# Separate in and out buffers on GpSimd's queue, state copies on VectorE, other PSUM banks for transposes, and a new order of scaling, tables and weights in a hybrid diffusion block

## The chip, the cores and the metric

The kernel runs on one core of a Trainium2 chip. The metric is device microseconds for one execution of the whole program; three runs of the kernel before took 2377.81 to 2379.08 us, with a median of 2378.53. Engines in the profile: PE is TensorE's matmul and PEld its weight load, DVE is VectorE, ACT is ScalarE, POOL is GpSimd, SP is SyncE, which issues nearly all DMAs here.

## The reference

One layer over 2048 latent tokens of 1024 channels and 256 context tokens, all float32. A token mixer comes first, then a channel mixer:

```python
sh1, sc1, g1, sh2, sc2, g2 = modulation(c, w_mod, b_mod)           # silu(c) @ w_mod + b_mod
zc = modulate(rmsnorm(hc, norm1_g), csh1, csc1) @ w_in             # context
zx = modulate(rmsnorm(h, norm1_g), sh1, sc1) @ w_in                # latent: S5 part, conv part
stx_f = s5_scan(ux, disc_f, h0_f, False)                           # 32 groups of 16, 64 complex states
stx_b = s5_scan(ux, disc_b, h0_b, True)                            # starts from the context's state
mix = concatenate([s5_mixer(ux, stx_f, stx_b, ...),                # C h + D u, GELU, GLU
                   conformer_conv(zx[..., 512:], ...)])            # GLU, depthwise conv 31, LayerNorm, swish
h = h + g1 * (mix @ w_out)
h = h + g2 * conv_ffn(h, ...)   # up to 2 x 2816, depthwise conv 3 and SiLU on the gate, product, down
return rmsnorm(h, final_g)
```

## The kernel before

Activations lie with channels on the partitions, in four tiles q = 0 to 3 of 512 tokens. Each float32 matmul is made of three float32r matmuls (`mm3`): weight and input are split into a high part, cast by ScalarE (`wH`, `x0H`, `x1H`), and a low part, the difference, by VectorE (`wL`, `x0L`, `x1L`). One output tile of 128x512 with an inner size of 512 is twelve matmuls.

The work is in stages.

Stage 1, to about 310 us. `xload` and `xstat` (together `stat(q)`) load a tile and find its reciprocal root mean square; `xapply` (`app(q)`, lines 235 to 247) scales it on VectorE and splits it. `s5_pass` and `conf_block` multiply by `w_in`. Meanwhile VectorE builds the S5 tables: 16 calls of `win_tab` (products at line 427, transposed by PE into the cv banks, written to `WI_d`) and 8 of `wall_tab` (line 452, to `WA_d` and `KC_d`). `win_tabs(n)` makes the next n of the 16. The order of these calls is at lines 686 to 703.

Stage 2, to about 470 us. The S5 input matmuls (line 755), VectorE's scan over blocks of 16 steps (lines 788 to 791), the rest of the modulation (`mod_block`, streamed `w_mod`) and of `conf_block`.

Stage 3, to about 670 us. 16 rounds, one for each pair of groups: eight copies of states from `S` into `h0` and `h1` (lines 838 and 842; buffers named hr, two of each), eight matmuls into an ax bank (lines 847 to 850), a copy of the bank into `yt` (line 855); after each fourth round PE transposes `yt` and ScalarE applies GELU (lines 861 to 863). Three steps of the convolution `conv_all` are taken after each round: `conv_in` transposes the gated input (line 561), `conv_mm` multiplies by banded Toeplitz tiles (line 575), `conv_out` transposes back (line 589). S5 and the convolution's transposes take turns in the same two ax banks.

Stage 4, to about 735 us. `mix_glu` for four tiles, and `layer_norm` over the convolution's output.

Stage 5, to about 990 us. `out_half(n, qs, ts_)` multiplies the mix by one half of `w_out`, over eight output blocks m and two tiles q: 64 tiles in all. For each, `xb` (three buffers) takes the residual (for n = 0 from the input, for n = 1 the partial sum `P_d`), VectorE adds the gated product in place, and GpSimd's queue stores it to `P_d` or `H_d`. `t_prep` (pass 0) runs beside the third `out_half`: from `H_d` it makes the seven operands T of a Strassen-like product and writes them to `T_d`; `t_load` reads and splits them.

Stage 6, from about 990 to 1866 us. Two passes p of 22 `unit`s. A unit loads and combines its weights (`left`: two loads into `wr`, which has four buffers, four splits, four sums), then makes seven products (`prod`) of twelve matmuls in the order B11, T2, B21, T1, T3, B22, T4. In the last unit of pass 0 each product is followed by `t_load` of the same operand for pass 1.

Stage 7, to the end. The down projection (`down`, line 1129), which adds into the held tiles, and the final norm.

The context is made with `schedule_with_timeline_sim=True`: a planner in the compiler orders the instructions on each engine and the DMAs on each queue by an estimate of when each is ready, with the order of the program as priority. So neighbours in the program need not be neighbours in the trace; but once laid out, each engine and each queue runs its list in order, and an instruction that waits holds up all behind it.

Of the kernel before, what the change touches and what calls it, by code (L numbers as in the profile page):

```python
# [9 lines left out]
FT = mybir.dt.float32  # L10
# [34 lines left out]
def tile_block(ctx, tc, xl, cxl, wmod, cols, s5p, dcol, eye, win, wglu, wout, wup, wdn, toep, out):  # L45
# [22 lines left out]

    def ps_ax():
        return pp_["ax"].tile([128, 512], FT, name="ax")  # L70

    def ps_fl():
        return pp_["fl"].tile([128, 512], FT, name="fl")
# [341 lines left out]
    def win_tab(d, gb):  # L415
        g0 = d * 32 + gb * GB
        wt = tbu.tile([128, 1024], FT, name="wt", bufs=1)
        for i, g2 in enumerate((g0, g0 + 2)):
            ta = tbu.tile([128, 2, 256], FT, name="wa", bufs=2)
            tc_ = tbu.tile([128, 2, 256], FT, name="wb", bufs=1)  # L420
            x = []
            for tl, lam, bb in ((ta, LR, BA), (tc_, LI, BB)):
                e = lam[:, 0:16, g2:g2 + 2].rearrange("p e g -> p g e")
                if d == 1:
                    e = e[:, :, ::-1]
                o = tl[:, :, :256]
                V.tensor_tensor(o.rearrange("p g (c e) -> p g e c", e=16),
                                e.unsqueeze(3).to_broadcast([128, 2, 16, 16]),
                                bb[:, g2:g2 + 2, :].unsqueeze(2).to_broadcast([128, 2, 16, 16]), op=OP.mult)
                x.append(o)  # L430
            V.tensor_tensor(x[0], x[0], x[1], op=OP.add)
            ps = pp_["cv"].tile([128, 512], FT, name="cv")
            for g in range(2):
                for k in range(2):
                    TE.transpose(ps[:, (g * 2 + k) * 128:(g * 2 + k + 1) * 128],  # L435
                                 ta[:, g, k * 128:(k + 1) * 128], ident)
            A.copy(wt[:, i * 512:(i + 1) * 512], ps)
        SY.dma_start(WI_d[d, gb], wt)
# [113 lines left out]
    def conv_in(n, q, gt):  # L552


        g2 = wp.tile([128, 1024], FT, name="wr", bufs=4)
        SY.dma_start(g2, G_d[q, n])
        for h in range(2):
            pt = ps_ax()
            for r in range(4):
                o = (4 * h + r) * 128  # L560
                TE.transpose(pt[:, r * 128:r * 128 + 128], g2[:, o:o + 128], ident)
            A.copy(gt[:, 8 * q + 4 * h:8 * q + 4 * h + 4, :], pt.rearrange("p (r i) -> p r i", r=4))
            yield
# [19 lines left out]
    def conv_out(n, co, las):  # L583

        for q in range(NQ):
            for h in range(2):
                pt = ps_ax()
                for r in range(4):
                    TE.transpose(pt[:, r * 128:r * 128 + 128], co[:, :, 8 * q + 4 * h + r], ident)
                for s in range(2):  # L590
                    A.activation(las[q][:, 2 * n + s, 256 * h:256 * h + 256].rearrange("p (r w) -> p r w", w=W),
                                 pt.rearrange("p (r s w) -> p s r w", r=4, s=2)[:, s], AF.Identity,
                                 bias=col("cb", 2 * n + s))
                yield
# [16 lines left out]
    def layer_norm(q, hs):  # L611
# [1 line left out]
        a = las[q]  # L613

        def col_mean(f):
            w = cf.tile([128, 2, TQ], FT, name="pt", bufs=2)
            V.tensor_tensor(w, f(0), f(1), op=OP.add)
            ts_ = cf.tile([128, TQ], FT, name="lsum", bufs=1)
            V.tensor_tensor(ts_, w[:, 0], w[:, 1], op=OP.add)
# [63 lines left out]
    def app(q, x, rb):  # L683
        X[q] = xapply(q, *x, rb)
# [1 line left out]
    cr = ctx_mm(ctx_scale(*xc, rbc, 0))  # L686
    app(2, x2, rb2)
    s3 = stat(3)
    win_tabs(2)
    ctx_out(cr)  # L690
    app(3, *s3)
    s0 = stat(0)
    win_tabs(4)
    s5_pass((2, 3))
    s1 = stat(1)
    win_tabs(4)
    for j in range(4):
        conf_block(j, (2, 3))
    app(0, *s0)
    app(1, *s1)  # L700
# [39 lines left out]
    for gb in range(NB):  # L740
# [7 lines left out]
        for i in range(2):  # L748
            a = gb * 2 + i
            for d in range(2):  # L750
                ps = ps_ax() if d == 0 else pp_["cv"].tile([128, 512], FT, name="cv")
                for ri in range(2):
                    for k in range(2):
                        for b in range(2):
# [62 lines left out]
    for a in range(16):  # L817
# [17 lines left out]
        h0 = so.tile([128, 2, NL], FT, name="hr0", bufs=2)  # L835
        for ri in range(2):
            for b in range(2):
                A.copy(h0[ri * 64:ri * 64 + 64, b, :], S[b * 64:b * 64 + 64, 0, a, ri, NC_ - 1:NC_ - 1 + NL])
        h1 = so.tile([128, 2, NL], FT, name="hr1", bufs=2)
        for ri in range(2):  # L840
            for b in range(2):
                A.copy(h1[ri * 64:ri * 64 + 64, b, :], S[b * 64:b * 64 + 64, 1, a, ri, 1:1 + NL])  # L842
        ps = ps_ax()
        for g in range(2):
            o = ps[:, g * 256:(g + 1) * 256]
# [77 lines left out]
    def out_half(n, qs, ts_):  # L923
# [3 lines left out]
        for m in range(KT):  # L927
# [4 lines left out]
                wh, wl = split_w(wr)  # L932
            o = 512 * (m % 2)
            for q, t in zip(qs, ts_):
                xb = lp.tile([128, TQ], FT, name="xb", bufs=3)
                SY.dma_start(xb, (P_d if n else xl)[q, :, m, :])
                ps = ps_mm()
                for k in range(4):
                    c = slice(o + 128 * k, o + 128 * k + 128)
                    mm3(ps, wh[:, c], wl[:, c], t[:, 0, k], t[:, 1, k], k == 0, k == 3)  # L940
                V.scalar_tensor_tensor(xb, ps, mod[:, 16 + m, 0:1], xb, op0=OP.mult, op1=OP.add)  # L941
                P.dma_start((H_d if n else P_d)[q, :, m, :], xb)  # L942
                if n == 0:
                    continue
# [90 lines left out]
    def left(i):  # L1035
# [16 lines left out]
        vs = split(v[:, 512:])  # L1052
        return gs_, s12s, s34s, vs

    def unit(i, p, nxt=None):
        gw, s12, s34, vw = left(i)

        def prod(ps, w, o, b, first=True, last=True):
            wh, wl = w
# [6 lines left out]
                TE.matmul(ps, lhsT=wl[:, c], rhs=t[:, 0, k], start=False, stop=e, skip_group_check=True)  # L1066
            if nxt is not None:
                t_load(nxt, b)

        def new(name, bufs):  # L1070
            return po.tile([128, TQ], FT, name=name, bufs=bufs)
# [258 lines left out]
```

## Time and profile before

| | before |
|---|---|
| median of three runs | 2378.53 us |
| the profiled execution, its own time | 2375.49 us |
| its span, first to last instruction | 2373.7 us |
| PE busy | 2198.7 us (93%) |
| PEld busy | 1758.8 us (74%) |
| VectorE busy | 1638.5 us (69%) |
| ScalarE busy | 830.9 us (35%) |
| GpSimd busy | 49.9 us (2%) |
| mean granted TensorE clock | 0.957 |
| DMA traffic | 349.7 MB, 147 GB/s in the mean |

The profile is that of one execution, whose time of its own is 3.0 us under the median; outside the span lie 1.8 us. Busy PE says that a matmul was in flight, not that it ran at its peak: the clock says at which of its two levels it ran. Times in the rows are microseconds from the start of the span, unless ns is said.

### The profile page before, as it was taken

The numbers are of one execution on the slowest core, as the hardware profiler recorded it, in microseconds if no ns is written. First come the engines' busy times: TensorE is split into PE (matmuls) and PEld (weight loads), VectorE is DVE, ScalarE is ACT, GpSimd is POOL, SyncE is SP. The second block draws the span as 40 slices with busy tenths as digits, with TensorE's granted clock in tenths as the row PEclk, the third lists the DMA queues.
The fourth block names the chain that finished last, engine by engine and source line by source line (L and its number), as shares of the span: only waits on it lengthen the run. The fifth ranks groups of instructions, "written<-read, shape, count | busy, mean of one in ns | idle before, by whom it ended". The sixth has DMA issues, their size and how long they took to land.

```text
span 2373.7 us, 28855 instructions
## 1 busy us (share of the span) xinstructions
PE 2198.7 (93%) x10958; PEld 1758.8 (74%) x10958; DVE 1638.5 (69%) x2506; ACT 830.9 (35%) x1221; POOL 49.9 (2%) x83
## 2 busy tenths in 40 slices
PE   6899999887887967899999997999999999999996
PEld 3678777576765845688778886888888888888885
DVE  9893578830256566677697768777777787788775
ACT  3452311145364433343343344333333311132113
POOL 0000000000000101100000000000000000000002
PEclk9999999979798978899999998999999999999998
DMA  8552586676424679522363234222222732334311
GB/s 321 177 153 89 143 276 228 228 223 185 129 90 172 204 261 318 197 80 89 116 213 97 80 110 148 89 85 83 91 80 80 265 126 80 106 107 144 105 54 71
DMA packets 178683, 349.70 MB, mean 147 GB/s; under 512 B 54512, under 2 KB 82544, under 8 KB 178032
## 3 DMA queue, kind: packets, MB, share of 16 engines
q1 hardware_dynamic: 173424, 331.07, 43.0%
q0 software_dynamic: 5120, 16.78, 1.8%
q8 instruction: 86, 1.41, 0.2%
q14 instruction: 53, 0.43, 0.1%
HBM read 252.45 MB, written 95.35 MB: 147 GB/s over the span
## 4 chain that ended last, share of the span: by engine, by line
issue 65%; PE 23%; DMA 5%; ACT 3%; DVE 2%; POOL 1%; SPq 0%; POOLq 0%; ACTq 0%; DVEq 0%
PE mm L182 5%; PE mm L183 4%; PE mm L184 4%; PE mm L575 2%; PE ax L847 1%; PE cv L755 1%; DMA xb<-P_d 1%; PE ax L755 1%; DMA xr<-in_xl 1%; PE ax L154 1%; PE fl L468 1%; ACT hr L842 1%; POOL P_d L942 1%; PE ax L849 1%; PE cv L435 1%
## 5 line engine op out<-in xcount | busy, mean ns | idle before, releaser
L183 PE MATMUL mm<-bh,bd 128*128 128x512 f32 (+1 forms) x720 | 277.4, 385 | 0.0
L184 PE MATMUL mm<-bh,bd 128*128 128x512 f32 (+1 forms) x720 | 277.1, 385 | 0.0
L182 PE MATMUL mm<-bh,bd 128*128 128x512 f32 (+1 forms) x720 | 274.4, 386 | 0.0
L1064 PE MATMUL mm<-t,wH 128*128 128x512 f32 x528 | 207.9, 394 | 18.0 <-ACT wH L1031 17.4
L1066 PE MATMUL mm<-t,wL 128*128 128x512 f32 x528 | 207.4, 393 | 0.5 <-DVE wL L1032 0.5
L1065 PE MATMUL mm<-t,wH 128*128 128x512 f32 x528 | 207.0, 392 | 0.0
L183 PEld LDWEIGHTS mm<-bh,bd 128*128 128x128 f32 x720 | 135.3, 188 | 27.4 <-issue 0.7
L182 PEld LDWEIGHTS mm<-bh,bd 128*128 128x128 f32 x720 | 135.3, 188 | 27.3 <-DVE x1H L1129 0.2
L184 PEld LDWEIGHTS mm<-bh,bd 128*128 128x128 f32 x720 | 135.3, 188 | 27.0 <-issue 0.2
L1116 ACT CAST bd<-wr 128x1024 fp32r<-128x1024 f32 x44 | 46.2, 1050 | 306.2 <-PE mm L184 296.1
L1031 ACT CAST wH<-sr 128x1024 fp32r<-128x1024 f32 x88 | 92.6, 1054 | 164.0 <-PE mm L1065 143.8
L1032 DVE TENSOR_TENSOR wL<-sr,wH 128x1024 fp32r<-128x1024 f32 x88 | 107.4, 1221 | 55.7 <-ACT wH L1031 55.7
L183 PE MATMUL mm<-x0L,wH 128*128 128x512 f32 (+1 forms) x352 | 139.6, 397 | 0.2 <-DVE x0L L494 0.2
L182 PE MATMUL mm<-x1H,wH 128*128 128x512 f32 x320 | 130.7, 408 | 8.3 <-DVE xb L941 8.3
L1064 PEld LDWEIGHTS mm<-t,wH 128*128 128x128 f32 x528 | 100.4, 190 | 39.8 <-ACT wH L1031 18.2
L184 PE MATMUL mm<-x1H,wL 128*128 128x512 f32 x320 | 128.2, 401 | 0.0
L1031 ACT CAST wH<-wr 128x1024 fp32r<-128x1024 f32 (+1 forms) x88 | 73.6, 837 | 154.4 <-PE mm L1065 143.3
L1066 PEld LDWEIGHTS mm<-t,wL 128*128 128x128 f32 x528 | 100.1, 190 | 22.8 <-DVE wL L1032 1.9
L1065 PEld LDWEIGHTS mm<-t,wH 128*128 128x128 f32 x528 | 100.3, 190 | 20.8
L1100 DVE TENSOR_TENSOR c<-mm,u 128x512 f32<-128x512 f32 x44 | 30.4, 691 | 120.8 <-PE mm L1066 120.7
L1129 DVE SCALAR_TENSOR_TENSOR x1L<-mm,mod,x1L 128x512 f32<-128x512 f32 (+1 forms) x96 | 66.9, 705 | 42.5 <-PE mm L184 42.5
L1129 DVE SCALAR_TENSOR_TENSOR x0L<-mm,mod,x0L 128x512 f32<-128x512 f32 x88 | 65.5, 750 | 41.3 <-PE mm L184 41.2
(349 smaller groups left out, 4980.1 us busy)
## 6 DMA issues: line engine op xcount, KB each, us to landing
wr<-in_wup SPq DMA_DIRECT2D x88, 512.0 KB
Y_d<-ft SPq DMA_DIRECT2D x88, 256.0 KB
wr<-in_wdn SPq DMA_DIRECT2D x44, 512.0 KB
wr<-Y_d SPq DMA_DIRECT2D x44, 512.0 KB
mw<-in_wmod SPq DMA_DIRECT2D x32, 512.0 KB
wr<-T_d SPq DMA_DIRECT2D x28, 512.0 KB
wr<-in_win SPq DMA_DIRECT2D x26, 512.0 KB
u<-U_d SPq DMA_DIRECT2D x32, 288.0 KB
```

Of the source, the lines that this page charges most:

```text
L182: TE.matmul(ps, lhsT=wh, rhs=xh, start=first, stop=False)
L183: TE.matmul(ps, lhsT=wh, rhs=xlo, start=False, stop=False)
L184: TE.matmul(ps, lhsT=wl, rhs=xh, start=False, stop=last)
L575: TE.matmul(pp[s][r, 32 * i:32 * i + 32], lhsT=tv[r, i, :], rhs=gt[r, :, 16 * c + i], start=True, stop=True, tile_position=(64 * s, 64 * s ...
L755: sil = TE.matmul(ps[64 * b:64 * b + 64, ri * NK:(ri + 1) * NK], lhsT=wi[d][:, 2 * i + b, k, ri * 64:(ri + 1) * 64], rhs=u[:, k, 2 * i + b ...
L1031: A.copy(h[:, :n], raw)
L1032: V.tensor_tensor(l[:, :n], raw, h[:, :n].bitcast(FT), op=OP.subtract)
L1064: TE.matmul(ps, lhsT=wh[:, c], rhs=t[:, 0, k], start=f, stop=False, skip_group_check=True)
L1065: TE.matmul(ps, lhsT=wh[:, c], rhs=t[:, 1, k], start=False, stop=False, skip_group_check=True)
L1066: TE.matmul(ps, lhsT=wl[:, c], rhs=t[:, 0, k], start=False, stop=e, skip_group_check=True)
L1116: A.copy(t[:, 0], wr)
L1129: V.scalar_tensor_tensor(h, ps, mod[:, 40 + m, 0:1], h, op0=OP.mult, op1=OP.add)
```

## The change

It has five parts:

- `out_half` loads the residual into buffers `xi` of their own (three), on GpSimd's queue instead of SP's, and VectorE writes the sum into `xb` (now two buffers), which is stored as before. `pt` of `layer_norm` has one buffer instead of two.
- The copies of states into `h0` and `h1` are VectorE's instead of ScalarE's.
- The transposes of `conv_in` and `conv_out` go to the two cv banks instead of the two ax banks. (`ps_cv` is a name for what was written out.)
- In stage 1, `app(3)` is followed by `s5_pass((2, 3))`, which has no tables ahead of it any more; `stat(0)` comes after that, and `win_tabs` are spread by twos between the calls of `conf_block`. The number of tables is the same.
- In the last unit of pass 0, the weights of unit 0 of pass 1 (`left(0)`) are prepared right after the second product and its `t_load`, and handed over through the list `pre`.

```diff
@@ -68,6 +68,9 @@
 
     def ps_ax():
         return pp_["ax"].tile([128, 512], FT, name="ax")
+
+    def ps_cv():
+        return pp_["cv"].tile([128, 512], FT, name="cv")
 
     def ps_fl():
         return pp_["fl"].tile([128, 512], FT, name="fl")
@@ -429,7 +432,7 @@
                                 bb[:, g2:g2 + 2, :].unsqueeze(2).to_broadcast([128, 2, 16, 16]), op=OP.mult)
                 x.append(o)
             V.tensor_tensor(x[0], x[0], x[1], op=OP.add)
-            ps = pp_["cv"].tile([128, 512], FT, name="cv")
+            ps = ps_cv()
             for g in range(2):
                 for k in range(2):
                     TE.transpose(ps[:, (g * 2 + k) * 128:(g * 2 + k + 1) * 128],
@@ -555,7 +558,7 @@
         g2 = wp.tile([128, 1024], FT, name="wr", bufs=4)
         SY.dma_start(g2, G_d[q, n])
         for h in range(2):
-            pt = ps_ax()
+            pt = ps_cv()
             for r in range(4):
                 o = (4 * h + r) * 128
                 TE.transpose(pt[:, r * 128:r * 128 + 128], g2[:, o:o + 128], ident)
@@ -584,7 +587,7 @@
 
         for q in range(NQ):
             for h in range(2):
-                pt = ps_ax()
+                pt = ps_cv()
                 for r in range(4):
                     TE.transpose(pt[:, r * 128:r * 128 + 128], co[:, :, 8 * q + 4 * h + r], ident)
                 for s in range(2):
@@ -613,7 +616,7 @@
         a = las[q]
 
         def col_mean(f):
-            w = cf.tile([128, 2, TQ], FT, name="pt", bufs=2)
+            w = cf.tile([128, 2, TQ], FT, name="pt", bufs=1)
             V.tensor_tensor(w, f(0), f(1), op=OP.add)
             ts_ = cf.tile([128, TQ], FT, name="lsum", bufs=1)
             V.tensor_tensor(ts_, w[:, 0], w[:, 1], op=OP.add)
@@ -686,15 +689,18 @@
     cr = ctx_mm(ctx_scale(*xc, rbc, 0))
     app(2, x2, rb2)
     s3 = stat(3)
-    win_tabs(2)
     ctx_out(cr)
     app(3, *s3)
+    s5_pass((2, 3))
+    win_tabs(2)
     s0 = stat(0)
-    win_tabs(4)
-    s5_pass((2, 3))
+    conf_block(0, (2, 3))
+    win_tabs(2)
+    conf_block(1, (2, 3))
+    win_tabs(2)
     s1 = stat(1)
-    win_tabs(4)
-    for j in range(4):
+    for j in (2, 3):
+        win_tabs(2)
         conf_block(j, (2, 3))
     app(0, *s0)
     app(1, *s1)
@@ -748,7 +754,7 @@
         for i in range(2):
             a = gb * 2 + i
             for d in range(2):
-                ps = ps_ax() if d == 0 else pp_["cv"].tile([128, 512], FT, name="cv")
+                ps = ps_ax() if d == 0 else ps_cv()
                 for ri in range(2):
                     for k in range(2):
                         for b in range(2):
@@ -835,11 +841,11 @@
         h0 = so.tile([128, 2, NL], FT, name="hr0", bufs=2)
         for ri in range(2):
             for b in range(2):
-                A.copy(h0[ri * 64:ri * 64 + 64, b, :], S[b * 64:b * 64 + 64, 0, a, ri, NC_ - 1:NC_ - 1 + NL])
+                V.tensor_copy(h0[ri * 64:ri * 64 + 64, b, :], S[b * 64:b * 64 + 64, 0, a, ri, NC_ - 1:NC_ - 1 + NL])
         h1 = so.tile([128, 2, NL], FT, name="hr1", bufs=2)
         for ri in range(2):
             for b in range(2):
-                A.copy(h1[ri * 64:ri * 64 + 64, b, :], S[b * 64:b * 64 + 64, 1, a, ri, 1:1 + NL])
+                V.tensor_copy(h1[ri * 64:ri * 64 + 64, b, :], S[b * 64:b * 64 + 64, 1, a, ri, 1:1 + NL])
         ps = ps_ax()
         for g in range(2):
             o = ps[:, g * 256:(g + 1) * 256]
@@ -932,13 +938,14 @@
                 wh, wl = split_w(wr)
             o = 512 * (m % 2)
             for q, t in zip(qs, ts_):
-                xb = lp.tile([128, TQ], FT, name="xb", bufs=3)
-                SY.dma_start(xb, (P_d if n else xl)[q, :, m, :])
+                xi = lp.tile([128, TQ], FT, name="xi", bufs=3)
+                P.dma_start(xi, (P_d if n else xl)[q, :, m, :])
                 ps = ps_mm()
                 for k in range(4):
                     c = slice(o + 128 * k, o + 128 * k + 128)
                     mm3(ps, wh[:, c], wl[:, c], t[:, 0, k], t[:, 1, k], k == 0, k == 3)
-                V.scalar_tensor_tensor(xb, ps, mod[:, 16 + m, 0:1], xb, op0=OP.mult, op1=OP.add)
+                xb = lp.tile([128, TQ], FT, name="xb", bufs=2)
+                V.scalar_tensor_tensor(xb, ps, mod[:, 16 + m, 0:1], xi, op0=OP.mult, op1=OP.add)
                 P.dma_start((H_d if n else P_d)[q, :, m, :], xb)
                 if n == 0:
                     continue
@@ -1052,8 +1059,10 @@
         vs = split(v[:, 512:])
         return gs_, s12s, s34s, vs
 
+    pre = []
+
     def unit(i, p, nxt=None):
-        gw, s12, s34, vw = left(i)
+        gw, s12, s34, vw = pre.pop() if pre else left(i)
 
         def prod(ps, w, o, b, first=True, last=True):
             wh, wl = w
@@ -1066,6 +1075,8 @@
                 TE.matmul(ps, lhsT=wl[:, c], rhs=t[:, 0, k], start=False, stop=e, skip_group_check=True)
             if nxt is not None:
                 t_load(nxt, b)
+                if b == T2:
+                    pre.append(left(0))
 
         def new(name, bufs):
             return po.tile([128, TQ], FT, name=name, bufs=bufs)
```

## Rows read from the trace of the kernel before

**Rows 1.** Page, part 1: busy time, share of the span and instructions by engine.
```profile
PE 2198.7 (93%) x10958; PEld 1758.8 (74%) x10958; DVE 1638.5 (69%) x2506; ACT 830.9 (35%) x1221; POOL 49.9 (2%) x83
```
**Rows 2.** Stretches: length, busy time of each engine, TensorE clock, DMA share, GB/s.
```profile
86.00:108.00 22.00, 14.09 (x55) 9.51 (x56) 20.01 (x32) 10.49 (x19) 0.00 (x0) 0.77 0.69 183
...
471.00:530.00 59.00, 52.69 (x600) 47.59 (x600) 24.92 (x50) 26.00 (x64) 0.00 (x0) 0.71 0.74 229
530.00:669.00 139.00, 112.79 (x882) 94.63 (x883) 22.45 (x27) 67.59 (x184) 0.00 (x0) 0.86 0.47 145
...
757.00:773.00 16.00, 9.10 (x22) 4.84 (x21) 10.33 (x14) 9.19 (x10) 0.54 (x1) 0.68 0.71 240
...
879.00:905.00 26.00, 19.23 (x69) 15.23 (x69) 17.51 (x25) 7.48 (x10) 2.65 (x5) 0.81 1.02 358
905.00:948.00 43.00, 33.27 (x129) 25.43 (x128) 26.21 (x27) 18.82 (x20) 5.17 (x11) 0.92 0.88 301
...
1422.00:1446.00 24.00, 8.54 (x26) 6.12 (x27) 21.60 (x26) 14.18 (x17) 0.00 (x0) 0.72 0.77 246
1446.00:2348.00 902.00, 901.32 (x4027) 746.81 (x4026) 676.82 (x919) 269.47 (x342) 0.20 (x1) 1.00 0.31 102
```
**Rows 3.** PE's waits, whole span: who waited for whom, us, times, longest.
```profile
PE mm L182 <- ACT wH L172: 26.6, 4, 15.0
...
PE mm L182 <- DVE xb L941: 13.9, 8, 3.4
...
PE ax L561 <- ACT x0H L562: 5.3, 3, 2.7
...
PE ax L861 <- ACT yt L855: 4.4, 4, 1.5
...
PE ax L589 <- ACT yt L855: 3.5, 4, 1.1
```
**Rows 4.** Chain of waits that ended last, near 81 us: start, length, what.
```profile
81.29 7.14 DMA xr<-in_xl
```
**Rows 5.** VectorE in order of time, 80 to 97 us: start, length, what.
```profile
81.99 0.17 DVE L118 RECIPROCAL stt<-stt 128x4 f32<-128x4 f32 x1
...
96.69 0.75 DVE L235 SCALAR_TENSOR_TENSOR xr<-xr,gs,ax 128x512 f32<-128x512 f32 x1
```
**Rows 6.** Line 838 alone (842 is alike): ns min/median/max.
```profile
L838 ACT COPY hr<-S x64: 294/297/300, 473.7 to 654.6; 64x128 f32<-64x128 f32 x64
```
**Rows 7.** VectorE's copies of lines 763 and 764: ns min/median/max.
```profile
L763 DVE COPY S<-cv x16: 417/422/426, 316.1 to 374.6; 128x256 f32<-128x256 f32 x16
L764 DVE COPY S<-cv x16: 179/181/184, 316.5 to 375.0; 128x32 f32<-128x32 f32 x16
```
**Rows 8.** SP queue's waits, 735 to 990 us: us, times, longest.
```profile
SPq L936 <- DMA H_d<-xb: 74.2, 29, 6.6
SPq L936 <- DMA P_d<-xb: 64.1, 22, 6.9
```
**Rows 9.** SP queue in order of time, 735 to 775 us, merged.
```profile
735.47 26.84 SPq L936 DMA_DIRECT2D xb<-in_xl  x11
762.41 8.28 SPq L930 DMA_DIRECT2D wr<-in_wout  x6
```
**Rows 10.** Line 942 alone, GpSimd's stores: ns each; landing in us.
```profile
L942 POOL DMA_DIRECT2D P_d<-xb x32: 539/539/710, 739.6 to 937.0; - x32
...
DMA to landing us min/median/max: 2.2/3.6/7.0
```
**Rows 11.** PE in order of time at the pass change; idle before it, releaser.
```profile
1440.45 0.79 PE L1064 MATMUL mm<-t,wH 128*128 128x512 f32 x1 [14.32 <-ACT wH L1031]
```
**Rows 12.** VectorE in order of time at the pass change.
```profile
1439.16 1.23 DVE L1021 TENSOR_TENSOR x1L<-wr,x1L 128x1024 fp32r<-128x1024 f32 x1 [1.78 <-ACT x1L L1020]
```
**Rows 13.** VectorE by line, 1400 to 1462 us: count, busy us, mean ns.
```profile
L1032 DVE TENSOR_TENSOR wL<-sr,wH 128x1024 fp32r<-128x1024 f32 x4 | 4.9, 1224 | 0.6 <-ACT wH L1031 0.6
...
L1045 DVE TENSOR_TENSOR sr<-wr 128x512 f32<-128x512 f32 x3 | 2.1, 687 | 0.0
```

## The prediction, made before the changed kernel ran

> **What bounds the kernel now.** The page's first part comes first: TensorE (PE) is busy for 2198.7 us of a span of 2373.7, VectorE for 69%, ScalarE for 35%, GpSimd for 2% [rows 1]. So PE sets the end, and what can be won is its idle time, 2373.7 - 2198.7 = 175 us, and what it does at the lower clock. The table of stretches says where that lies [rows 2]: from 1446 to 2348 us PE stands still for 0.7 us of 902, so nothing that only lightens another engine there is worth anything. That row also gives the pace, 4027 matmuls in 902 us, 0.224 us each at the full clock, so 2.69 us for a tile of twelve. The holes lie in five places: 86 to 108 us (22.0 - 14.1 = 7.9 us idle), 471 to 530 (6.3), 530 to 669 (26.2), 735 to 998 (the output projection; 6.9 us in the stretch from 757 to 773 and 9.7 in that from 905 to 948 alone), and 1422 to 1446 (15.5). The rest, at the start, the tail and in small pieces between, isn't touched. PE's list of waits names who ended the holes [rows 3], and I take the edits by those names.
>
> **Scaling ahead of tables (86 to 108 us).** Edit: app(3) and the first s5_pass come ahead of the first two win_tabs, and stat(0) behind s5_pass. Nothing is removed; all 16 win_tabs stay to be done somewhere. In the chain of waits a load for stat(0) runs from 81.3 to 88.4 us [rows 4]; ScalarE and VectorE then finish that statistic while PE's next matmuls wait, although they need only tile 3's rsqrt. VectorE began that rsqrt at 81.99 and the scaling by it at 96.69, with tables and stat(0) between [rows 5]. The four small steps and two transposes need some 3 us by themselves, so up to 10 us could come forward. The hole is 7.9 us, and at a mean clock of 0.77 the 14.1 us of work in it lose about 14.1 x 0.23 = 3 more: at most 11. Against it: the order on each engine is a planner's, which fills VectorE with tables whenever it thinks it free, wherever they are written. I take 6, bounds -6 (the same hole again, elsewhere) and 11.
>
> **Copies on VectorE, transposes in other banks (471 to 669 us).** ScalarE loses 128 copies of 0.297 us [rows 6], 38 us of the 93.6 that it is busy in the two stretches [rows 2]. Eight of them, 2.4 us, stand in each of the 16 rounds around the copy of yt out of PSUM, and PE waits for yt and for the convolution's copies by name: 5.3 + 4.4 + 3.5 us in the three largest rows [rows 3]. The 3.5 (a convolution transpose that waits for S5's yt) is purely the shared pair of ax banks, and goes with the new banks. Of the 5.3, ScalarE's copies in the way are most; of the 4.4 (yt itself) two thirds. Then 3.5 + 4 + 3 = 10.5; smaller waits of the same kind and clock regained (0.86 in that stretch) give 2.5. I take 13 of the 32.5 us idle; bounds 5 (the bank wait and little else) and 20. VectorE's price is not in the trace for this shape: between 0.18 us (128x32) and 0.42 us (128x256, out of PSUM) [rows 7]; I take 0.25, nearer the small one, since 128 elements lie nearer to 32. That is 32 us, bounds 23 and 54, beside 47 us of work in 198, so VectorE's idle time hides it. Were that cover gone, the matmuls that read the copies would be late, and then yt.
>
> The Trainium skill has a price for these copies (VectorE: DVE Perf Modes, section The TRN2 errata): 58 cycles and one per element at 0.96 GHz, as an estimate 0.19 us for 128 elements; for ScalarE its 224 and one per element at 1.2 GHz come to 0.293, and the trace shows 0.297. By it VectorE would get 25 us more, not 32, and the sum would be the same.
>
> **Loads on GpSimd's queue, buffers of their own (735 to 998 us).** Before, one of three buffers xb holds a load, the sum and the store, and the load goes out on SP's queue only once an earlier store has landed: SP stands waiting for stores of xb for 74.2 + 64.1 = 138 us [rows 8], and everything behind stands too. From 735.47 on eleven such loads take 26.8 us of the queue, and only then are the next weights of wout asked for, at 762.41 [rows 9]. PE's hole from 757 to 773 ends with those weights. After, the eleven are elsewhere; the weights can be there before PE is. Idle 6.9 us, and 9.1 us of work at a clock of 0.68 loses about 3: I take 8, bounds 3 and 10.
>
> From 905 to 948 PE waits for xb itself (most of the 13.9 us that it waits for it in all [rows 3]). A load there waits for a landing. After, it waits only for the sum that last read its buffer, and the store has two buffers: sum 0.75, issue 0.3, landing 3.6 in the middle and 7.0 at worst [rows 10], halved: 2.3 to 4.0 us a tile, against 2.69 for PE. At about 5.3, between the two, it is 3.2. Ten tiles went by in 43 us, 4.3 each; ten times 1.1 is 11. The DMA share is 0.88 there, so I take 7, bounds 0 and 11. PE's longest wait for wout's weights, 15.0 of 26.6 us [rows 3], lies between these two stretches, from 863 to 878, but there SP's queue is full of t_prep's stores and the DMA share is 1.02 from 879 to 905 [rows 2]; I take 3, bounds 0 and 12. The rest of the stage, 2. Together 20, bounds 3 and 32. GpSimd gets 64 issues of 0.539 us [rows 10], 35 us, hidden by its idleness. That col_mean has one buffer costs nothing: both steps that use it are VectorE's, in order.
>
> **left(0) early (1422 to 1446 us).** PE starts pass 1 at 1440.45 after 14.3 us of waiting for wH [rows 11], so pass 0 ended at 1426.1. The weights' load stands behind the reloads of all seven T tiles in the same four buffers. After, it is asked for after the second. Then what is late next is the last T tile: its split ended at 1440.39 [rows 12], and before it now stand four splits, one of half width, and four sums of left(0), about 3 x 1.22 + 0.7 + 4 x 0.69 = 7.1 us [rows 13], so 1447.5. PE, starting at 1426, wants it six products later, 1426 + 6 x 2.69 = 1442.1. It waits 5.4 us instead of 14.3: 9 won, and 2 of clock (mean 0.72 there). I take 11, bounds 4 and 17.
>
> **Sum.** 6 + 13 + 20 + 11 = 50. The planner lays out all queues anew; two of the holes above (7.9 and 6.9 us) are its own misjudgements of what comes first, and I charge one such new hole with its lost clock, 9. So 41 us. The profiled execution took 2375.5 (span 2373.7), 3.0 below the median of the runs, 2378.5; 2334.5 on its scale is **2338 us** on the median's. Under 0.2%, 4.8 us, a measurement can't tell it from no change.
>
> **Rivals.**
> A. GpSimd's queue is in order and the loads run no further ahead than the stores (slower). A load of the next tile that stands behind a store which waits for the sum costs, for each tile, 0.75 + 0.3 + 0.54 + 0.54 + 3.6 = 5.7 us. 64 tiles are 365 us where the stretch of [rows 8], 255 us, holds them today: +110, less the 30 of the other edits, +9 for the new hole: 2468. With the loads one tile ahead it is half, 2.9, and no loss; so it decides whether they run ahead at all. For it: the queue's stores all wait for sums today. Against: the eleven loads in a row on SP [rows 9] were laid out ahead as far as buffers went. Chance 0.06.
> B. The order hardly changes, since the planner took what was ready already: the first and last edits give nothing. 13 + 20 - 9 = 24: 2354. For it: tables are spread as filler far from where they are written [rows 5]. Chance 0.2.
> C. The stores' landing becomes the bound, at 4.0 us a tile in the DMA-heavy part, and the output stage gains nothing: 2358; with a second new hole and the transposes at their low bound, 8 + 9 less, 2375. Together 0.1.
> D. VectorE's work holds GpSimd back: each issue starts after a split of 1.22 us [rows 13], so two issues take 2 x (0.54 + 1.22) = 3.5 us a tile, 0.8 more than PE's 2.69; if half of the tiles run at PE's pace, 32 x 0.8 = 26 of the 41 are gone, 2364. Against: all 64 stores took 0.539, 0.71 at most [rows 10]. Chance 0.03. The Trainium skill (SBUF — State Buffer, section SBUF: two separate sides) says that a VectorE operation that uses both ports keeps GpSimd from writing descriptors, which speaks against moving loads to this queue; the stores' row shows no such delay.
> E. The forecast, 2316 to 2356: 0.58. Better than that, 0.03.
>
> Faster: 0.58 + 0.03 + 0.2 + 0.06 (of C) + 0.02 (of D) = 0.89, less 0.04 for bounds that fall together: 0.85. Same 0.05 (rest of C and D). Slower 0.1: A, and the low bounds of the first two edits with a second hole (-6, 5, 3, 4, less 18). The range of 8 in 10 goes from 2314 to 2370.
>
> **What would show it.** Right: SP's waits for stores gone and wout's loads not behind them; no PE wait for a convolution transpose on yt; ScalarE about 38 us less busy; the hole at the pass change about 5 us, ended by a T tile; VectorE up by some 32 us; the span from 1446 to the end unchanged. Wrong: GpSimd's queue waiting between loads for sums, PE waiting for xb more than 13.9 us, a new hole before 420 us for tables, or left(0)'s splits holding the T tiles past 1450.

## The result and the profile after

The changed kernel takes 2310.74 us, the median of four runs (2307.22 to 2312.52); the kernel before, on the same chip, 2378.81 (2377.81 to 2382.6). The ratio is 0.9709, 95% interval 0.9692 to 0.9726: 69 us faster, where 41 were forecast and the range ended at 2314. The profiled execution took 2312.18 us, its span 2310.4.

Part 1 of the page after, beside [rows 1]:

```profile
PE 2186.4 (95%) x10958; PEld 1751.5 (76%) x10958; DVE 1665.6 (72%) x2634; ACT 793.0 (34%) x1095; POOL 84.3 (4%) x147
```

ScalarE lost 37.9 us (38 forecast), GpSimd gained 34.4 (35), VectorE 27.1 for 128 copies (32). PE's idle time fell from 175 to 124 us, and PE itself is 12.3 us less busy for as many matmuls.

Stretches after (columns as in [rows 2]); each row answers to one there, or to several:

```profile
86.00:108.00 22.00, 15.17 (x58) 9.63 (x59) 19.83 (x32) 10.45 (x19) 0.00 (x0) 0.77 0.71 196
...
712.00:729.00 17.00, 9.75 (x34) 5.84 (x33) 13.12 (x13) 8.85 (x11) 3.22 (x6) 0.81 0.57 185
824.00:850.00 26.00, 13.96 (x48) 10.96 (x48) 17.52 (x27) 9.05 (x13) 2.38 (x5) 0.67 0.98 321
850.00:875.00 25.00, 16.14 (x61) 12.91 (x61) 12.12 (x15) 7.10 (x8) 4.30 (x8) 0.80 0.94 346
1374.00:1398.00 24.00, 21.32 (x94) 17.05 (x93) 22.65 (x27) 15.71 (x19) 0.00 (x0) 1.00 0.78 255
```

The hole at the tables is nearly as deep as before (6.8 us idle, 7.9 before, the clock still 0.77). The holes in the output projection have mostly moved, to 712 to 729 and 824 to 875, the latter with a DMA share still near 1; from VectorE's first sum to the end of the stage PE is idle for 50.6 us (248.9 long), where it was for 54.7 (256.8 long). The pass change has 2.7 us idle at the full clock, where it had 15.5 at 0.72.

The largest saving lies outside these stretches, between the scan and `mix_glu`, from 450 us to ScalarE's first split for the GLU. First before, then after:

```profile
450.00:666.90 216.90, 180.32 (x1561) 147.66 (x1560) 58.91 (x126) 93.66 (x247) 0.00 (x0) 0.83 0.57 179
```

```profile
450.00:631.20 181.20, 172.34 (x1559) 143.52 (x1557) 86.41 (x252) 53.66 (x120) 0.00 (x0) 0.83 0.67 213
```

The matmuls are as many but for two, and the stretch is 35.7 us shorter: 27.7 of it is idle time (36.6 to 8.9), and 8.0 is time with a matmul in flight. The forecast for this stage was 13.

PE's waits after, whole span, as in [rows 3]:

```profile
PE mm L185 <- ACT wH L175: 24.6, 3, 13.4
...
PE mm L185 <- DVE xb L948: 10.2, 8, 2.8
...
PE fl L624 <- DVE lsum L622: 4.5, 2, 4.1
```

The waits for wout's weights (`wH`) and for `xb` are a little smaller (by 2.0 and 3.7 us); the rows of the convolution's transposes are gone from the list.

### The profile page after: what moved, and what is told of

It is laid out like the page before. It is cut to its first block, busy times and chain, and to the rows that moved or that the text cites. A ratio compares the mean times of both kernels' runs of the same rounds, so it can differ in the third digit from the quotient of the medians.

```text
span 2310.4 us, 28840 instructions
## 1 busy us (share of the span) xinstructions
PE 2186.4 (95%) x10958; PEld 1751.5 (76%) x10958; DVE 1665.6 (72%) x2634; ACT 793.0 (34%) x1095; POOL 84.3 (4%) x147
## 4 chain that ended last, share of the span: by engine, by line
PE 62%; issue 22%; DMA 9%; DVE 4%; ACT 2%; POOL 1%; SPq 0%; DVEq 0%; POOLq 0%; ACTq 0%
PE mm L1075 11%; PE mm L1073 11%; PE mm L1074 11%; PE mm L185 6%; PE mm L186 5%; PE mm L187 5%; PE mm L578 3%; DMA H_d<-xb 2%; PE ax L853 1%; PE ax L157 1%; PE cv L761 1%; PE ax L761 1%; DMA xr<-in_xl 1%; DMA wr<-T_d 1%; DMA wr<-in_toep 1%
## 5 line engine op out<-in xcount | busy, mean ns | idle before, releaser
L185 PEld LDWEIGHTS mm<-bh,bd 128*128 128x128 f32 x720 | 135.3, 188 | 27.1 <-DVE x1H L1140 0.2
L187 PEld LDWEIGHTS mm<-bh,bd 128*128 128x128 f32 x720 | 135.3, 188 | 27.1 <-issue 0.2
L1038 ACT CAST wH<-wr 128x1024 fp32r<-128x1024 f32 x88 | 73.6, 837 | 151.8 <-PE mm L1074 143.3
```

What stands on the lines that cost most here:

```text
L185: TE.matmul(ps, lhsT=wh, rhs=xh, start=first, stop=False)
L187: TE.matmul(ps, lhsT=wl, rhs=xh, start=False, stop=last)
L1038: A.copy(h[:, :n], raw)
```

## The experiments

Each kernel was timed in three rounds beside the kernel before. Gains are by the ratio, in us of 2378.5, with the 95% interval in brackets.

| kernel | median, us | ratio | gain on before, us |
|---|---|---|---|
| the whole change | 2310.7 | 0.9709 | 69 (65 to 73) |
| p_banks | 2338.4 | 0.9834 | 39 (36 to 43) |
| p_copy | 2347.9 | 0.9878 | 29 (25 to 32) |
| p_xi | 2361.1 | 0.9932 | 16 (12 to 20) |
| p_pre | 2365.7 | 0.9950 | 12 (8 to 15) |
| p_ord | 2378.0 | 1.0010 | -2 (-5 to 0) |
| p_bankcopy | 2333.5 | 0.9826 | 41 (36 to 47) |
| p_cvin | 2348.7 | 0.9883 | 28 (22 to 34) |
| p_cvin0 | 2367.4 | 0.9955 | 11 (7 to 15) |
| p_cvin1 | 2361.4 | 0.9929 | 17 (13 to 21) |
| p_cvout | 2360.4 | 0.9935 | 15 (11 to 20) |
| a_min | 2310.4 | 0.9715 | 68 (64 to 71) |
| a_nocopy | 2311.6 | 0.9722 | 66 (61 to 71) |
| a_noord | 2311.9 | 0.9732 | 64 (57 to 71) |
| a_noxi | 2324.5 | 0.9783 | 52 (48 to 55) |
| a_xisp | 2316.5 | 0.9752 | 59 (54 to 64) |
| a_woutp | 2313.6 | 0.9724 | 66 (62 to 70) |
| a_tstp | 2326.9 | 0.9779 | 53 (48 to 57) |
| a_xi2xb3 | 2322.5 | 0.9769 | 55 (51 to 59) |

**One part at a time.** Five kernels take one part of the change each; the hunks are those of the diff above.

p_banks:

```diff
-            pt = ps_ax()        # conv_in, and the same in conv_out
+            pt = ps_cv()
```

> The kernel before with one part of the change alone: the convolution's transposes in the cv banks. Theory: this part carries most of what stage 3 gained (35.7 us), because until the scan ends one of the two ax banks is the scan's and the other goes round among the modulation blocks, so that the convolution could not begin; in cv banks it begins about 17 us earlier and fills the rounds' gaps later: 20 to 36 us faster, first convolution transpose near 455 instead of 472. Rival (the prediction's split): ScalarE's copies in the rounds were the brake, and the banks alone give what PE waited for yt in convolution transposes, 4 to 8 us.

p_copy:

```diff
-                A.copy(h0[...], S[...])        # and the same for h1
+                V.tensor_copy(h0[...], S[...])
```

> The kernel before with the state copies on VectorE and nothing else. Theory (banks): the copies alone give 3 to 10 us, since the convolution still begins only after the scan. Rival (ScalarE was the brake): 13 to 36 us faster. Both: ScalarE 38 us less busy, VectorE 23 to 54 us more.

p_xi:

```diff
-                SY.dma_start(xb, (P_d if n else xl)[q, :, m, :])
+                P.dma_start(xi, (P_d if n else xl)[q, :, m, :])     # xi 3, xb 2, pt 1 buffers
```

> The kernel before with the loads of the output projection on GpSimd's queue in buffers of their own (and the single pt buffer), nothing else. Prediction: 20 us faster in that stage. Theory after seeing the changed kernel: 6 to 11 us, since its holes for wout's weights (24.6 us against 26.6) stayed. Rival: SP's waits of 138 us were worth more, and another part of the change took it back: 20 us here.

p_pre:

```diff
+                if b == T2:
+                    pre.append(left(0))
```

> The kernel before with left(0) prepared inside the last unit of pass 0, nothing else. Theory: the hole of 14.3 us at the pass change closes but for 1 to 3 us: 12 to 16 us faster. Prediction: 5.4 us of waiting for a T tile remain, 11 us faster. Rival: the planner had taken what was ready: no change.

p_ord:

```diff
     app(3, *s3)
+    s5_pass((2, 3))
+    win_tabs(2)
     s0 = stat(0)
-    win_tabs(4)
-    s5_pass((2, 3))
...
```

> Edit: the kernel before with the new order of stage 1 alone (scaling and the first S5 product ahead of the tables). The prediction's step: 6 us gained, 2372. Theory after the traces: the planner puts the tables where it thinks VectorE free, PE resumes with tile 3 at 100.8 to 101.5 us as before, and the time is within 5 us of 2378.5. Rival: the order costs something later (the scan's end comes later), 5 to 10 us more, which the other edits of the change hide.

The banks give 39 us, the copies 29, the buffers and the queue 16, the early weights 12, the order nothing. The singles come to 94 us, 25 more than the whole. So some of them win the same time, and the next runs ask which.

**Banks and copies.** p_bankcopy has both edits. p_cvin and p_cvout have the new banks in one step of the convolution each, p_cvin0 and p_cvin1 in `conv_in` for one half of the channels each:

```diff
-            pt = ps_ax()
+            pt = ps_ax() if n else ps_cv()      # p_cvin0; p_cvin1: ps_cv() if n else ps_ax()
```

> Edit: the kernel before with the convolution's transposes in the cv banks and the state copies on VectorE, nothing else. Alone the banks gave 40 us and the copies 31. Theory: both fill the same holes between the scan's end and the first mixer matmul, so that together they give little more than the banks alone: 36 to 48 us, about 2335, the convolution's first transpose near 455 us and the GLU's first matmul near 630. Rival, the holes are separate (banks: the early start of the convolution; copies: the length of a round): 60 to 71 us, about 2312, the GLU's first matmul near 610; then the loss of 33 us between the singles' sum and the whole lies in other edits.

> Edit: the kernel before with conv_in's transposes alone in the cv banks; conv_out's stay in the ax banks. Theory: most of the banks' 40 us come from the convolution's beginning before the scan lets go of the ax banks (first transpose at 457 instead of 471 us), which this run has: 28 to 40 us, about 2344. Rival, the wait of conv_out's transposes on the copy of yt inside the rounds is what the banks remove: at most 15 us, 2363 or more, although the first transpose begins as early.

> Edit: the kernel before with conv_out's transposes alone in the cv banks; conv_in's stay in the ax banks. Theory (the early start is what counts): the first transpose stays at 471 us and the time falls by 0 to 10 us, 2368 to 2378. Rival (the wait of conv_out's transposes on yt inside the rounds): 20 us or more, 2358 or less. The step of the prediction that it tests gave 3.5 us for that wait.

> Edit: the kernel before with conv_in's transposes in the cv banks for the first half of the channels alone (n = 0, those around the scan's end); the second half's stay in the ax banks. Both halves together gave 28 us. Theory, early start: most of it is won here, since the transposes begin 15 us before the scan lets go of its bank: 18 to 26 us, 2351 to 2359. Rival, the bank waits inside the rounds, from 550 to 582 us, carry as much as the start: 12 to 16 us, about 2363.

> Edit: as the run before it, but the second half of the channels alone (n = 1, inside the rounds) in the cv banks; the first half's stay in the ax banks and can't begin early. Theory, early start: 3 to 9 us, 2368 to 2374. Rival, the waits in the rounds: 12 to 16 us, about 2363.

Both together give 41 us, and 39 + 29 = 68 don't appear: the copies add 2 to the banks, within the error. In the banks' run the same stretch shows why:

```profile
450.00:630.10 180.10, 169.60 (x1569) 140.41 (x1567) 60.48 (x131) 91.56 (x247) 0.00 (x0) 0.85 0.68 219
```

With ScalarE as busy as before (91.6 us, 93.7 before), PE's idle time is down from 36.6 to 10.5 us. There is little left for the copies to win.

Whose waits went is seen in the list of groups by line, for the same stretch. Before (L561 is `conv_in`, L589 `conv_out`, L861 the transpose of `yt`; behind the second bar stands PE's idle time ahead of the group, and what ended it):

```profile
L589 PE MATMUL ax<-ident,x1H 128*128 128x128 f32 x64 | 11.6, 315 | 6.9 <-ACT yt L855 3.5 <-ACT x1L L591 3.1 <-ACT S L863 0.2
L561 PE MATMUL ax<-ident,wr 128*128 128x128 f32 x64 | 10.5, 302 | 11.5 <-ACT x0H L562 5.3 <-ACT x0L L562 2.4 <-ACT yt L855 2.1
L861 PE MATMUL ax<-ident,yt 128*128 128x128 f32 x64 | 9.6, 292 | 8.6 <-ACT yt L855 4.4 <-ACT S L863 4.1
```

and with the banks alone (the same lines are 592, 564 and 864):

```profile
L592 PE MATMUL cv<-ident,x1H 128*128 128x128 f32 x64 | 10.8, 311 | 1.3 <-ACT x1L L594 1.2
...
L864 PE MATMUL ax<-ident,yt 128*128 128x128 f32 x64 | 10.0, 301 | 4.8 <-ACT yt L858 3.3 <-ACT S L866 1.6
L564 PE MATMUL cv<-ident,wr 128*128 128x128 f32 x64 | 9.1, 277 | 0.8 <-ACT x0L L565 0.8
```

27.0 us of waiting became 6.9, though no copy of ScalarE was moved. The copies alone (p_copy) do the same, though no bank was changed; the stretch and the three groups there:

```profile
450.00:640.80 190.80, 171.98 (x1556) 140.82 (x1554) 85.87 (x250) 54.85 (x119) 0.00 (x0) 0.86 0.63 201
```

```profile
L589 PE MATMUL ax<-ident,x1H 128*128 128x128 f32 x64 | 10.5, 292 | 2.0 <-ACT yt L855 0.8 <-ACT x1L L591 0.8 <-ACT S L863 0.4
L561 PE MATMUL ax<-ident,wr 128*128 128x128 f32 x64 | 9.4, 284 | 1.2 <-ACT x0H L562 0.5 <-ACT yt L855 0.5 <-ACT S L863 0.2
...
L861 PE MATMUL ax<-ident,yt 128*128 128x128 f32 x64 | 9.2, 283 | 3.8 <-ACT yt L855 2.0 <-ACT S L863 1.8
```

Here 27.0 became 7.0. So these waits are one hole that either edit closes, and that is why the two don't add. A transpose that "waits for ScalarE's x0H" waits for the copy that empties the bank it is about to fill. Two banks serve three users (S5's products, the transposes of `yt`, the convolution's transposes), so this copy is soon waited for; it can be made to come earlier, with ScalarE relieved of the state copies, or to be needed later, with two more banks. No run let all three users share four banks, so it isn't shown that the pair must be the convolution's own.

What the banks win beyond the copies is in good part the early start: from 450 to 475 us PE is idle for 1.0 us with the banks alone and for 6.4 with the copies alone, 5.4 of the 8.3 us by which the two stretches differ in idle time.

The theory that most of the 39 us is the early start fell. The first half's transposes did come early, and moving them gives 11 us, in which their waits for their banks are counted too; the second half's, which begin long after the scan (at 528.6, 555.1 before), give 17, and `conv_out`'s in the rounds 15. The spans of `conv_in` (ns min/median/max, first and last start), p_cvin0 first, then p_cvin1:

```profile
L564 PE MATMUL cv<-ident,wr x32: 270/273/476, 453.8 to 464.7; 128*128 128x128 f32 x32
L564 PE MATMUL ax<-ident,wr x32: 272/273/329, 540.1 to 566.7; 128*128 128x128 f32 x32
```

```profile
L564 PE MATMUL ax<-ident,wr x32: 272/300/477, 470.9 to 481.2; 128*128 128x128 f32 x32
L564 PE MATMUL cv<-ident,wr x32: 272/273/329, 528.6 to 542.2; 128*128 128x128 f32 x32
```

Where they have the cv banks, the first half's transposes start at 453.8 instead of 470.9, and the second half's take 13.6 us from the first to the last instead of 26.6 (as in the kernel before).

**Parts taken out of the whole.** Each of these is the changed kernel with one part as before (a_noord, a_noxi, a_nocopy), or with both parts that seem to be worth nothing beside the others as before (a_min: order and copies). a_xisp moves one load back:

```diff
-                P.dma_start(xi, (P_d if n else xl)[q, :, m, :])
+                SY.dma_start(xi, (P_d if n else xl)[q, :, m, :])
```

> Edit: the changed kernel with stage 1 in the order of before. The order alone changed nothing on the kernel before (2378.0 beside 2377.0). Theory: it changes nothing here either, 2307 to 2314. Rival: in the changed kernel the order costs some 4 us, since the stretch from the last S5 input matmul to the first sum of the output projection is 326.4 us there and 322.3 with banks and copies alone; then 2304 to 2307.

> Edit: the changed kernel with the state copies on ScalarE as before. Theory: with the convolution's transposes in other banks PE is busy for 163 of 170 us from 450 to 620 us even with ScalarE's copies, so VectorE's copies add 3 us at most as they did on the kernel before (2333.5 beside 2338.4): 2310 to 2316. Rival: 10 us or more slower, 2321, the copies being worth a third of their 31 us when alone.

> Edit: the kernel before with three of the five edits: the convolution's transposes in other banks, xi and xb on GpSimd's queue with one pt, left(0) early; state copies on ScalarE and the order of stage 1 as before. Theory: these three carry all of the change, 2308 to 2314 (each of the other two undone by itself moved the changed kernel by 1 us). Rival: the copies and the order stand in for each other, so that without both 5 us or more are lost: 2316 or more.

> Edit: the changed kernel with xb in place, three buffers, on SP's queue, and two buffers pt, as before. Theory, the edits add up: 17 us slower, 2326 to 2330. Rival: within the whole the edit is worth less, since the output projection takes 248.9 us in the changed kernel against 255.5 with banks and copies alone, and 242.1 against 256.8 where this edit stands alone: 6 to 9 us slower, 2317 to 2320.

> Edit: the changed kernel with the loads of xi on SP's queue; buffers of their own stay. Theory, the queue matters: eleven such loads held SP's queue for 26.8 us before, 2.4 us each, and the weights of wout behind them come late again at the start of the stage: 5 to 12 us slower, 2316 to 2323, and PE waits for wH or lsum near 725 us longer. Rival, only the wait of a load for a store's landing mattered, and the own buffers end it on either queue: within 4 us of 2311.

Without the order, without the copies, and without both, the intervals hold the whole's 0.9709: three parts make the change. The buffers and the queue of xi are worth 14 us by the medians and 18 by the ratios, near the 16 that they gave alone, so they add to the rest. With its own buffers but on SP's queue the edit keeps about half of that; the intervals of a_xisp and of the whole don't meet. The reason given for it in the expectation doesn't hold, though. SP's queue after, in order of time, then in a_xisp:

```profile
723.23 8.40 SPq L936 DMA_DIRECT2D wr<-in_wout  x6
```

```profile
694.12 23.10 SPq L942 DMA_DIRECT2D xi<-in_xl  x11
722.81 8.39 SPq L936 DMA_DIRECT2D wr<-in_wout  x6
```

The weights of wout are asked for at the same time with the eleven loads ahead of them and without. Nor are the 23.10 us the cost of eleven issues: such a merged row runs from the first to the last, and by itself one takes 0.333 us in the median; the rest is waiting for buffers. What holds the weights' loads is in SP's list of waits after, from 690 to 760 us:

```profile
SPq L936 <- DVE pt L620: 33.4, 2, 29.7
```

It is `layer_norm`, whose sum into `pt` (line 620) still reads buffers wr that the weights need. What the 6 (medians) to 10 us (ratios) of the queue are made of, the runs don't tell.

**What paces the output projection.** Three trials on the changed kernel:

```diff
-                SY.dma_start(wr.rearrange("p (m x) -> p m x", m=2), ...)      # a_woutp
+                P.dma_start(wr.rearrange("p (m x) -> p m x", m=2), ...)
-                SY.dma_start(T_d[p, o, :, kk, :], t)                          # a_tstp
+                P.dma_start(T_d[p, o, :, kk, :], t)
-                xi = lp.tile([128, TQ], FT, name="xi", bufs=3)                # a_xi2xb3
+                xi = lp.tile([128, TQ], FT, name="xi", bufs=2)
-                xb = lp.tile([128, TQ], FT, name="xb", bufs=2)
+                xb = lp.tile([128, TQ], FT, name="xb", bufs=3)
```

> Edit: the changed kernel with the loads of wout's weights in the output projection on GpSimd's queue instead of SP's. PE's two largest waits that are left in that stage, 13.5 and 7.7 us near 836 and 858 us, end with such weights, whose loads stand behind stores to T_d on SP's queue. Theory, the place in SP's queue is what makes them late: 8 to 18 us faster, 2293 to 2303. Rival, the four buffers wr (shared with those stores) and the DMA engines, full at a share of 0.97 there, make them late on any queue: within 4 us of 2311.

> Edit: the changed kernel with the stores of T1 to T4 to T_d (32 in all over both passes, from the buffers sr) on GpSimd's queue instead of SP's. Theory, SP's queue makes wout's weights late near 836 and 858 us: 5 to 15 us faster, 2296 to 2306. Rival, the DMA engines are full there whatever the queue (share 0.97): within 4 us; or slower by 5 us where the loads of xi stand behind these stores on GpSimd's queue.

> Edit: the changed kernel with two buffers xi and three xb instead of three and two; the memory is the same. In the changed kernel VectorE's sums wait 25.6 us, 17 times, for a store of xb to land and 4.3 us, once, for a load of xi. Theory: the stores' landing, not the loads, now paces the DMA-heavy part, so PE's 10.2 us of waits for xb shrink and the time falls by 3 to 8 us: 2303 to 2308. Rival: loads two tiles ahead come late instead: 2311 or up to 10 us more.

None is faster. The weights on GpSimd's queue bring nothing (0.9724, not told from the whole): their first load is asked for at 722.2 instead of 723.2, their last at 893.9 instead of 894.1, and PE waits 22.1 us for `wH` instead of 24.6. So leaving SP's queue isn't enough to make them early; GpSimd's queue waits for the buffers wr too (7.4 us for `pt`, 6.2 for a store to `T_d`). Whether the buffers, the other queue's own waits or the full DMA engines then hold them, the runs don't say. With the T stores on GpSimd's queue this queue stands waiting for VectorE to make them (27.3 us in all), the loads of xi and the stores of xb behind them stand too, and 16 us are lost; PE waits 30.3 us for `wH` there instead of 24.6. That the one makes up the other isn't shown. The largest of these waits in a_tstp:

```profile
POOL T_d L1014 <- DVE sr L1007: 15.0, 3, 11.1
```

The third trial is the most telling. VectorE's waits ahead of the sum, after (us, times):

```profile
  DMA H_d<-xb: 18.0, 13
  PE mm L187: 16.7, 13
  DMA P_d<-xb: 7.6, 4
  DMA xi<-in_xl: 4.3, 1
```

and with two xi and three xb:

```profile
  DMA xi<-P_d: 24.3, 17
  DMA xi<-in_xl: 14.1, 7
  PE mm L187: 14.0, 10
```

The wait for a store's landing (25.6 us) is gone, and 38.4 us of waiting for loads stand in its place. The reading is that the queue runs in order: a load stands behind a store that waits for a sum, and with two buffers it can't be far enough ahead.

## Why the prediction was wrong, step by step

The direction was right. The step that failed is the term for the transposes and copies: 13 us, bounds 5 and 20, where the two edits measured 41. A time below 2316 had been given a chance of 0.03. The forecast was 28 us short, and 28 are missing there; what the other terms were off (8 and 4 too much, 1 too little, and 9 for a hole that didn't come) cancels but for 2. Three choices made it small.

1. The sum took 10.5 us from the three largest rows (5.3, 4.4 and 3.5). PE waits for 27.0 us ahead of the three kinds of transposes, and the rows that name `x0L`, `x1L` and `S` were left among the small ones. The banks alone took 20.1 us of this, the copies alone 20.0. So *"The 3.5 (a convolution transpose that waits for S5's yt) is purely the shared pair of ax banks"* fell too: with the copies alone this row is down to 0.8, as the row for `x0H`, which was given to ScalarE's copies, is gone with the banks alone. The releaser's name says who emptied the bank, not which of the two edits ends the wait.
2. The stretches began at 471 us, where the convolution begins before. That it could begin before was not asked. p_cvin0, where the first half does from 453.8 us on, gains 11 us.
3. 2.5 us were taken for smaller waits and the clock. In the banks' run PE is 10.7 us less busy for the same work (180.3 to 169.6), in the whole 8.0. How much of that is the clock stays open: its mean over the stretch is 0.83 before, 0.85 with the banks and 0.83 in the whole.

The copies on VectorE were priced well (0.25 us, bounds 0.18 and 0.42). The trace after has 0.223:

```profile
L844 DVE COPY hr<-S x64: 213/223/226, 483.7 to 618.0; 64x128 f32<-64x128 f32 x64
```

The row of the Trainium skill that the prediction used (VectorE: DVE Perf Modes, section The TRN2 errata) divides the elements by a mode's factor, which the prediction took as 1; so it gave 0.194 us as an estimate. The measurement is 15% above that, and the section itself says that this row comes out too short for a single operation. Nothing hung on it. But of what the copies win, 29 us by themselves, 27 is won by the banks as well.

**Tables (6, bounds -6 to 11): -2.** Rival B's mechanism held here. The planner kept VectorE's order, and the chain of waits still has a load into `xr` for a statistic from 81.20 us on, 7.11 long. VectorE after:

```profile
81.85 0.20 DVE L121 RECIPROCAL stt<-stt 128x4 f32<-128x4 f32 x1
...
91.26 0.15 DVE L124 SCALAR_TENSOR_TENSOR stt<-stt 128x4 f32<-128x4 f32 x1
...
96.81 5.34 DVE L238 SCALAR_TENSOR_TENSOR xr<-xr,gs,ax 128x512 f32<-128x512 f32 x8
```

Reciprocal and scaling begin where [rows 5] has them, to 0.14 us.

**Output projection (20, bounds 3 to 32): 16.** The sum was near, its parts were not, so that it came near is luck. The 8 us for the hole from 757 to 773 rested on *"PE's hole from 757 to 773 ends with those weights"*. Only its last 2.4 us do. PE's waits from 735 to 773 us before, then from 705 to 735 us after:

```profile
PE fl L621 <- DVE lsum L619: 4.1, 1, 4.1
...
PE mm L182 <- ACT wH L172: 2.4, 1, 2.4
...
PE fl L621 <- DVE x0H L632: 0.4, 1, 0.4
```

```profile
PE fl L624 <- DVE lsum L622: 4.1, 1, 4.1
PE fl L624 <- DVE x0H L635: 3.1, 1, 3.1
```

The rest was `layer_norm`'s already, with the same 4.1 us for `lsum`. After, the weights' 2.4 are gone, 2.7 more are waited for `x0H`, and the hole is as long (7.3 us idle from 712 to 729). Nor could the weights come much earlier: the first call for them comes at 723.23, 23.5 us after the first sum, when `pt` frees their buffer; before it came 23.9 us after it, and `pt`'s read of such a buffer had ended only 2.4 us sooner, at 759.99. The 3 for the hole from 863 to 878 came to 2: the longest wait for these weights is 13.4 us, 15.0 before. The 7 for `xb` came to 5: in p_xi's stage PE's waits for `xb` fell from 13.9 to 8.9 us, those for `hacc`, which is summed from `xb`, from 9.9 to 6.2, those for `wH` from 26.6 to 23.6, 11.7 together. Of C (the landing becomes the bound) a part is true, as the 25.6 us of waits for stores show. A didn't come, since the loads run ahead; a_xi2xb3 shows its mechanism, and that the third buffer decides, for 12 us by the medians. D has nothing for it: GpSimd's loads took what its stores took in [rows 10], with VectorE busy for 156.8 of the stage's 248.9 us:

```profile
L942 POOL DMA_DIRECT2D xi<-in_xl x32: 538/538/714, 696.4 to 882.0; - x32
L942 POOL DMA_DIRECT2D xi<-P_d x32: 538/538/538, 748.7 to 932.4; - x32
```

The rule that D drew on (the Trainium skill, SBUF — State Buffer, section SBUF: two separate sides) shows in none of these 64 issues. They hardly test it, though: the operation that the section names as using both ports is a float32 copy within SBUF, and VectorE runs none from 690 to 935 us.

**Weights early (11, bounds 4 to 17): 12.** Right in size, and the last T tile is later than wanted as foretold, but by 0.7 us and not by 5.4. Pass 1 now begins at 1380.25, right behind pass 0; six products of 2.69 us later is 1396.39, and the tile's split ends at 1397.06. VectorE after, and then PE:

```profile
1395.84 1.22 DVE L1028 TENSOR_TENSOR x1L<-wr,x1L 128x1024 fp32r<-128x1024 f32 x1
```

```profile
1380.02 0.39 PE L1075 MATMUL mm<-x1L,wL 128*128 128x512 f32 x1
1380.25 0.39 PE L1073 MATMUL mm<-t,wH 128*128 128x512 f32 x1
...
1393.08 0.47 PE L1073 MATMUL mm<-x1H,wH 128*128 128x512 f32 x1 [1.80 <-DVE u L1106]
...
1396.93 0.50 PE L1073 MATMUL mm<-t,wH 128*128 128x512 f32 x1 [0.89 <-ACT wH L1038]
...
1397.51 0.39 PE L1073 MATMUL mm<-x1L,wH 128*128 128x512 f32 x1
```

PE reads the tile from 1397.51 on. In place of the waits of 14.3 and 1.3 us around the pass change stand 1.80 and 0.89, ended by `u` and by `wH`, not by the T tile as forecast, and the clock is 1.00 from 1374 to 1398.

**One new hole (9): none.** The measured parts come to 41 + 16 + 12 - 2 = 67, the whole to 69 (65 to 73): the parts add, once banks and copies are counted as one.

## What to carry to other kernels

When PE waits for the copy that empties a bank, count the users of that pair of banks and add up the waits by the line that waits, the small rows too, not by the name that ended them: other banks and an earlier copy can each end the same wait, here 20 of 27 us. Two edits that fill the same hole are worth little more than the larger of the two, so price them together, and bound a stage by all the idle time and lost clock that it has, from where its first step could start. A load on another queue is early only if its buffer is free as early: look who last held the buffer before counting what stands ahead in the queue.

## What was not expected of the hardware

GpSimd's queue is no cheaper place for an issue: 0.538 us in the median for a load of `xi`, where SP's queue took 0.333 for the same load in a_xisp; it is only the emptier one. And PE can have a matmul in flight without a break and be at the lower clock. In the changed kernel it is busy for all of 25 us, 14.5 of them with the convolution's 64x32 matmuls, at a granted clock of 0.63, so for most of them at the level of 1.2 GHz; in the 25 us ahead of that it was idle for 1.4 us and the clock was 0.96.

```profile
450.00:475.00 25.00, 23.62 (x225) 14.50 (x223) 13.28 (x49) 7.70 (x14) 0.00 (x0) 0.96 0.80 296
475.00:500.00 25.00, 25.00 (x225) 20.35 (x225) 17.48 (x50) 4.55 (x8) 0.00 (x0) 0.63 0.81 248
```
